# Memory products ordered by the half of the keys and values that they read, and three value blocks open at once

## The chip, the cores and the metric

The kernel runs on one NeuronCore of a Trainium2 chip. The metric is the device time of one execution in microseconds (us); three runs of the kernel before gave 1373.69, 1375.38 and 1381.63 us, with a median of 1375.38 us. The engines are TensorE (PE for the products, PEld for the weight loads that go with them), VectorE (DVE), ScalarE (ACT), GpSimd (POOL) and SyncE (SP), which here only issues DMAs.

## The reference, cut to what matters

One decoder layer over 1024 tokens of width 1024. It has a state-space mixer (S5), gated linear attention, cross-attention into 256 memory tokens, and a squared-ReLU MLP. The change touches the cross-attention alone:

```python
mem_n = layer_norm(mem, mem_ln_g, mem_ln_b)          # (256, 1024)
kv = mem_n @ w_kv
k = kv[..., :D_MODEL].reshape(bsz, MEM_LEN, MEM_HEADS, MEM_HEAD_DIM)   # 4 heads of 256
v = kv[..., D_MODEL:].reshape(bsz, MEM_LEN, MEM_HEADS, MEM_HEAD_DIM)
s = jnp.einsum('blhd,bmhd->bhlm', q, k) * (MEM_HEAD_DIM ** -0.5)       # q = x @ w_q
p = jax.nn.softmax(s, axis=-1)
o = jnp.einsum('bhlm,bmhd->blhd', p, v)
return o @ w_o
```

## The kernel before, in words

The memory does not depend on the tokens, so the kernel folds it into two matrices before it needs them. For each head it computes `A = w_q k^T` (stored in DRAM as `a_d`) and `VW = v w_o` (stored as `vw_d`); the attention later is `softmax(h A) VW`. The generator `mem_stream` does this head by head: it transposes `w_q` (`mem_wqT`), projects the memory to the keys (`mem_proj`), forms A in four blocks of 256 rows, projects the memory to the values (`mem_proj` again) and forms VW in four blocks of 128 x 512.

Every product that needs float32 precision is made of three. `split` cuts a matrix into a high half (ACT copies it in a shorter format) and a low half (DVE or POOL subtracts the high half from the source); `mm3` then adds high x high, high x low and low x high in one PSUM bank. Keys and values come out of `mem_proj` in the tile `kvT`: ACT writes the high half first, and DVE writes the low half behind it, both from the same PSUM bank. So the low half is late by whatever DVE has in front of it.

PSUM banks come from `bank(tag)`. Tag `"d"` has three of them, handed out in turn; a bank is free again when the last reader of its previous contents is done. The projection to the values has one of the three, and its last reader is the DVE subtraction that makes the low half.

The engines run their instructions in program order, each engine its own. That order is set when the program is built: a list scheduler takes instructions from the code as they become ready by its own estimate, so an edit in one place moves others near it, on every engine.

Head 0 runs at the start of the kernel. Around it the tokens are normalised and transposed, eight tiles of 128 tokens (`embed`: DVE, ACT and POOL share a layer norm, PE transposes, ACT and DVE split into `h0T`), each followed by a block of 24 products (`z_block`). DVE also has a long chain of tiny instructions on `prm` and `par` (128 x 16 and the like), which works out the coefficients of S5. Heads 1 to 3 run much later, mixed with the products of the gated unit and of the linear attention.

The lines that matter below: `mm3` (L168 to L171), `split` (L157 to L163), `mem_proj` (L352), `mem_stream` (L385).

Of the kernel before, what the change touches and what calls it, by code (L numbers as in the profile page):

```python
# [7 lines left out]
F32 = mybir.dt.float32  # L8
# [9 lines left out]
P = 128  # L18
# [63 lines left out]
def hybrid_layer(  # L82
# [8 lines left out]
    nc = tc.nc  # L91
# [3 lines left out]
    PE = nc.tensor  # L95

    x, mem, out = x[0], mem[0], out[0]
# [12 lines left out]
    vw_d = dram.tile([D, D], F32, name="vw_d")  # L110
# [10 lines left out]
    stage = ctx.enter_context(tc.tile_pool(name="stage", bufs=2))  # L121
    psp = ctx.enter_context(tc.tile_pool(name="psp", bufs=2, space=PSUM))

    def slot(name, shape, dtype=F32):
        return arena.tile(shape, dtype, tag="s", name=name)

    def bank(tag="d", shape=(P, 512)):
        return psp.tile(list(shape), F32, tag=tag, bufs={"d": 3, "s": 3, "g": 2}[tag], name="ps_" + tag)
# [26 lines left out]
    def act(o, i, f=AF.Copy, **kw):  # L155
        A.activation(out=o, in_=i, func=f, **kw)  # L156
# [7 lines left out]
            stt(V, lo, src, scale, hi.bitcast(F32), ALU.mult, ALU.subtract)  # L164

    P3 = ((0, 0), (0, 1), (1, 0))

    def mm3(o, lhs, rhs, first, last, more=False):  # L168

        for n, (i, j) in enumerate(P3):  # L170
            PE.matmul(o, lhs(i), rhs(j), start=first and n == 0, stop=last and n == 2, skip_group_check=more)  # L171
# [26 lines left out]
    def eng(bits, i):  # L198
        return V if bits >> i & 1 else G


    def weight(src, shape, e=nc.vector, hl=None):

        raw = rawp.tile(shape, F32, tag="raw", name="raw")
        nc.sync.dma_start(out=raw, in_=src)
        if hl is None:
            hl = wp.tile([P, 2] + list(shape[1:]), F32R, tag="w", name="hl")
        split(hl[:, 0], hl[:, 1], raw, e=e)
        return hl
# [57 lines left out]
    prm_s = slot("prm", [P, 4096])  # L267
# [20 lines left out]
    for b in range(4):  # L288
        z = (b + 1) % 3 * 512 + 512
        t = mrow[:, 0:2, :].rearrange("p a n -> p (a n)")[:, z:z + 512].rearrange("p (k m) -> p k m", k=2)  # L290
        for j in range(2):
# [3 lines left out]
            else:  # L295
# [11 lines left out]
                  in_=lst[64:80, :].unsqueeze(2).to_broadcast([16, 2, 64]))  # L307
# [41 lines left out]
    def mem_w(c0):  # L349
        bits = {0: MW, D: MV0}.get(c0, MV1 if c0 >= D else MW1)  # L350
        return [weight(w_mkv[kk * 512:(kk + 1) * 512, c0:c0 + 256].rearrange("(k p) n -> p k n", p=P), [P, 4, 256],
                       eng(bits, kk))  # L352
                for kk in range(2)]

    def mem_proj(ws):
        ps = bank("d", (P, 2, MEM))
        for dk in range(2):
            for k in range(8):
                mm3(ps[:, dk, :], lambda i: ws[k // 4][:, i, k % 4, dk * P:(dk + 1) * P],
                    lambda j: mnT[:, j, k, :], k == 0, k == 7)  # L360
            yield 2.6
        o = stage.tile([P, 2, 2, MEM], F32R, tag="kv", bufs=1, name="kvT")
        split(o[:, 0], o[:, 1], ps)
        return o

    def mem_load(h):
        ws = mem_w(h * 256)
        raws = []
        for ch in range(2):
            raw = rawp.tile([P, 4, 256], F32, tag="raw", name="wq")  # L370
            nc.sync.dma_start(out=raw, in_=w_mq[ch * 512:(ch + 1) * 512, h * 256:(h + 1) * 256]
                              .rearrange("(k p) n -> p k n", p=P))
            raws.append(raw)
        return ws, raws

    def mem_wqT(raw, tag):
        wq = wp.tile([P, 2, 2, 512], F32R, tag="w", name="wqT")
        for dk in range(2):
            ps = bank(tag, (P, 4, P))
            for ck in range(4):  # L380
                PE.transpose(ps[:, ck, :], raw[:, ck, dk * P:(dk + 1) * P], ident)
            split(wq[:, 0, dk, :], wq[:, 1, dk, :], ps.rearrange("p a c -> p (a c)"))
        return wq

    def mem_stream(heads, tag, room=None):  # L385
        nxt = mem_load(heads[0])
        yield 0
        for h in heads:
            ws, raws = nxt
            wq = [mem_wqT(raws[0], tag)]  # L390
            yield 0.9
            kT = yield from mem_proj(ws)
            wq.append(mem_wqT(raws[1], tag))
            ws = mem_w(D + h * 256)
            yield 0.9
            for r0 in range(0, D, 256):
                ps = bank("d", (P, 2, MEM))
                for c in range(2):
                    ck = r0 // P + c
                    for dk in range(2):  # L400
                        mm3(ps[:, c, :], lambda i: wq[ck // 4][:, i, dk, ck % 4 * P:(ck % 4 + 1) * P],
                            lambda j: kT[:, j, dk, :], dk == 0, dk == 1)
                st = stage.tile([P, 2, MEM], F32, tag="rt", bufs=3, name="ast")
                act(st, ps)
                nc.scalar.dma_start(out=a_d[r0:r0 + 256, h * 256:(h + 1) * 256].rearrange("(c p) m -> p c m", p=P),
                                  in_=st)
                yield 1.3
            wo = [weight(w_mo[h * 256:(h + 1) * 256, n * 512:(n + 1) * 512].rearrange("(k p) n -> p k n", p=P),
                         [P, 2, 512], eng(MO1 if room is None else MO0, n), None if room is None else room[:, n]) for n in range(2)]
            vT = yield from mem_proj(ws)  # L410
            if h != heads[-1]:
                nxt = mem_load(h + 1)
            yield 0
            for n in range(2):
                for mt in range(2):
                    ps = bank()
                    for dk in range(2):
                        mm3(ps, lambda i: vT[:, i, dk, mt * P:(mt + 1) * P], lambda j: wo[n][:, j, dk, :],
                            dk == 0, dk == 1)
                    z = (0, 512, 1792, 3456)[2 * n + mt]  # L420
                    st = (prm_s[:, z:z + 512] if room is not None and z
                          else stage.tile([P, 512], F32, tag="rt", bufs=3, name="vst"))
                    act(st, ps)
                    r0 = h * 256 + mt * P
                    nc.scalar.dma_start(out=vw_d[r0:r0 + P, n * 512:(n + 1) * 512], in_=st)
                    yield 1.3


    def z_block(w, tok, t, epi):
# [15 lines left out]
    def load_x(tk):  # L445
        nc.sync.dma_start(out=xs[tk // 4][:, tk % 4, :], in_=x[tk * P:(tk + 1) * P, :])

    fill = Filler(mem_stream([0], "g", slot("wo0", [P, 2, 2, 2, 512], F32R)))
    fill.run(F1)
    xs = [slot("xs0", [P, 4, D])]  # L450
# [86 lines left out]
    for th in range(2):  # L537
        po = bank()
        for k in range(8):
            for j in range(2):  # L540
                PE.matmul(po[0:32, :], wg[:, k, :], h0(k, j)[:, th * 512:(th + 1) * 512],
                          start=k == 0 and j == 0, stop=k == 7 and j == 1)
# [48 lines left out]
    def exp_parts(z):  # L591

        zc, n, r, em, sc, kk = etmp
        ex, ex1 = pt(), pt()
        ts(e, zc, z, 88.0, -90.0, ALU.min, ALU.max)
        ts(e, n, zc, LOG2E, MAGIC, ALU.mult, ALU.add)
        ts(e, n, n, MAGIC, op0=ALU.subtract)
        stt(e, r, n, -LN2H, zc, ALU.mult, ALU.add)
        stt(e, r, n, -LN2L, r, ALU.mult, ALU.add)
        ts(e, em, r, 1.0 / 5040)  # L600
        for c in (1.0 / 720, 1.0 / 120, 1.0 / 24, 1.0 / 6, 0.5, 1.0):
            stt(e, em, em, c, r, ALU.add, ALU.mult)
        ts(e, kk, n, 127.0, 0.0, ALU.add, ALU.max)
        ts(e, sc.bitcast(I32), kk, 8388608.0)
        stt(e, ex, em, 1.0, sc, ALU.add, ALU.mult)
        tt(e, em, em, sc, ALU.mult)
        stt(e, ex1, sc, -1.0, em, ALU.add, ALU.add)
        return ex, ex1
# [9 lines left out]
    step, _ = exp_parts(ls)  # L618
# [35 lines left out]
    n = 1  # L654
# [18 lines left out]
    for Et, cnt in ((E0, 16), (E1, 8)):  # L673
        G.memset(Et[:, 0, 0, :], 1.0)
        G.memset(Et[:, 1, 0, :], 0.0)
        n = 1
# [226 lines left out]
    def z_stream():  # L903
# [24 lines left out]
        for t in range(NT):  # L928
# [8 lines left out]
            yield 5.1  # L937

    mem_rest = mem_stream([1, 2, 3], "d")
    fill = Filler(z_stream(), mem_rest)  # L940
    fill.run(10)
# [48 lines left out]
    class Act:  # L990
# [8 lines left out]
        def lhs(self, k, i, t):  # L999
            return self(k // 4, t // 4)[:, i, k % 4, (t % 4) * P:(t % 4 + 1) * P]  # L1000

        def rhs(self, k, j, th):
            return self(k // 4, th)[:, j, k % 4, :]
# [406 lines left out]
    for _ in range(2):  # L1410
        z = wp.tile([P, 2, 2, 512], F32R, tag="w", name="w1q")
# [339 lines left out]
```

## Time and profile before

| | |
|---|---|
| median of three runs | 1375.38 us (1373.69 to 1381.63) |
| profiled execution | 1376.45 us, of which the span from first to last instruction is 1374.4 us |
| mean granted TensorE clock | 0.990 of 2.4 GHz |
| busy: PE, DVE, ACT, POOL | 97%, 70%, 41%, 30% of the span |

PE is busy nearly always, so time can be gained or lost only where it waits, or where its clock is at the lower level. The times in the sections below are microseconds from the start of the span.

### The profile page before, as it was taken

What the parts mean: (1) busy time and instruction counts of PE and PEld (TensorE: products, weight loads), DVE (VectorE), ACT (ScalarE), POOL (GpSimd) and SP (SyncE); (2) the same over time, 40 slices, a digit from 0 to 9 for tenths busy, and PEclk for the clock granted to TensorE, in tenths of its full rate; (3) what the DMA queues carried; (4) which work ended last, traced back from release to release, by engine and by line L of the source; (5) the groups of instructions that cost most, each with busy time, mean ns of one, the idle gap of its engine ahead of it and who ended that gap; (6) DMA issues with size and microseconds to landing.
All of it is one profiled execution on the core that took longest, in us unless ns stands there. A gap on an engine that the chain in (4) does not pass through costs nothing. (4 is left out here: it accounts for less than half of the span.)

```text
span 1374.4 us, 18808 instructions
## 1 busy us (share of the span) xinstructions
PE 1333.9 (97%) x6824; PEld 1108.2 (81%) x6824; DVE 968.6 (70%) x1713; ACT 569.6 (41%) x950; POOL 410.6 (30%) x315
## 2 busy tenths in 40 slices
PE   6799999999999999999999999999999999999997
PEld 6576788788898888788888788888887888888886
DVE  8999788756965379744379866665556576678785
ACT  4434433242545245333023754545556343344441
POOL 1654243311524123000013134443342143003363
PEclk9899999999999999999999999999999999999999
DMA  9832342543666220300112557644446983335332
GB/s 301 269 123 85 114 122 52 174 153 118 241 210 214 61 78 17 122 31 25 38 46 86 183 172 242 199 155 159 159 163 231 320 315 130 106 108 160 131 108 92
DMA packets 155512, 199.81 MB, mean 145 GB/s; under 512 B 16294, under 2 KB 86044, under 8 KB 155292
## 3 DMA queue, kind: packets, MB, share of 16 engines
q1 hardware_dynamic: 143536, 179.44, 40.1%
q10 hardware_dynamic: 11884, 19.17, 3.8%
q8 instruction: 54, 0.88, 0.3%
q14 instruction: 38, 0.31, 0.1%
HBM read 140.38 MB, written 58.20 MB: 144 GB/s over the span
## 5 line engine op out<-in xcount | busy, mean ns | idle before, releaser
L171 PE MATMUL ps_d<-xt,w1q 128*128 128x512 f32 x576 | 137.3, 389 | 0.7 <-DVE hid L150 0.7
L171 PEld LDWEIGHTS ps_d<-xt,w1q 128*128 128x128 f32 x576 | 108.1, 188 | 23.5 <-DVE hid L150 1.1
L171 PE MATMUL ps_s<-cell 128*128 128x512 f32 x432 | 113.0, 389 | 0.0
L171 PE MATMUL ps_d<-cell 128*128 128x512 f32 x432 | 106.0, 389 | 0.5 <-DVE hid L150 0.5
L171 PEld LDWEIGHTS ps_d<-cell 128*128 128x128 f32 x432 | 81.0, 188 | 17.7 <-DVE hid L150 0.9
L171 PEld LDWEIGHTS ps_s<-cell 128*128 128x128 f32 x432 | 81.1, 188 | 16.8
L156 ACT ACTIVATE hl<-raw 128x1024 fp32r<-128x1024 f32 x62 | 65.4, 1064 | 69.2 <-PE ps_d L171 63.1
L171 PE MATMUL ps_d<-hl,y 128*128 128x512 f32 x384 | 92.4, 395 | 0.0
L171 PE MATMUL ps_d<-hl,h0T 128*128 128x512 f32 x384 | 92.1, 397 | 0.3 <-DVE h0T L150 0.3
L171 PE MATMUL ps_g<-xb,w1q 128*128 128x512 f32 x384 | 92.1, 391 | 0.0
L171 PE MATMUL ps_d<-h0T,hl 128*128 128x512 f32 x384 | 90.8, 393 | 0.6 <-DVE hl L150 0.6
L171 PE MATMUL ps_d<-hl,p 128*128 128x512 f32 x384 | 89.0, 391 | 0.0
L171 PEld LDWEIGHTS ps_d<-h0T,hl 128*128 128x128 f32 x384 | 71.2, 188 | 19.9 <-issue 3.0
L156 ACT ACTIVATE hid<-hid 128x512 f32<-128x512 f32 x112 | 70.8, 632 | 39.0 <-DVE hid L150 37.2
L171 PEld LDWEIGHTS ps_d<-hl,h0T 128*128 128x128 f32 x384 | 72.0, 190 | 16.1 <-DVE h0T L150 0.7
L150 DVE TENSOR_TENSOR cell<-ha,cell 128x1024 fp32r<-128x1024 f32 x56 | 82.3, 1471 | 3.0 <-ACT cell L156 3.0
L171 PEld LDWEIGHTS ps_d<-hl,p 128*128 128x128 f32 x384 | 71.6, 188 | 14.6
L171 PEld LDWEIGHTS ps_g<-xb,w1q 128*128 128x128 f32 x384 | 71.5, 188 | 14.6
L150 DVE TENSOR_TENSOR hl<-raw,hl 128x1024 fp32r<-128x1024 f32 x50 | 68.5, 1381 | 20.7 <-ACT hl L156 20.2
L171 PEld LDWEIGHTS ps_d<-hl,y 128*128 128x128 f32 x384 | 70.7, 188 | 14.6 <-issue 0.3
L156 ACT ACTIVATE w1q<-raw 128x512 fp32r<-128x512 f32 x80 | 50.1, 629 | 69.9 <-PE ps_d L171 27.3
L150 POOL TENSOR_TENSOR hl<-raw,hl 128x1024 fp32r<-128x1024 f32 x12 | 33.8, 2823 | 144.0 <-ACT hl L156 144.0
(296 smaller groups left out, 2798.0 us busy)
## 6 DMA issues: line engine op xcount, KB each, us to landing
g_d<-hid SPq DMA_DIRECT2D x112, 256.0 KB
ha<-g_d SPq DMA_DIRECT2D x56, 512.0 KB
raw<-in_w_ff_dram SPq DMA_DIRECT2D x40, 512.0 KB
b<-in_w_ff_dram SPq DMA_DIRECT2D x32, 512.0 KB
raw<-in_w_mkv_dram SPq DMA_DIRECT2D x16, 512.0 KB
raw<-in_w_in_dram SPq DMA_DIRECT2D x16, 512.0 KB
wq<-in_w_mq_dram SPq DMA_DIRECT2D x8, 512.0 KB
xs<-in_x_dram SPq DMA_DIRECT2D x8, 512.0 KB
```

What stands on the lines that cost most here:

```text
L150: e.tensor_tensor(out=o, in0=a, in1=b, op=op)
L156: A.activation(out=o, in_=i, func=f, **kw)
L171: PE.matmul(o, lhs(i), rhs(j), start=first and n == 0, stop=last and n == 2, skip_group_check=more)
```

## The change

The four blocks of A and the four blocks of VW keep their products and their sums; the order of the products inside changes. `HI_FIRST` lists, for each block, first the four products that read the high half of `kvT` and then the two that read the low half. For VW the first three blocks are opened together: their twelve high products stand in front, then their six low products, then the fourth block alone. Three banks of tag `"d"` are therefore held at once. The numbers in `yield` are the amounts by which other work is interleaved.

```diff
+    HI_FIRST = ((0, 0, 0), (0, 1, 0), (1, 0, 0), (1, 1, 0), (0, 0, 1), (1, 0, 1))
...
                 for c in range(2):
                     ck = r0 // P + c
-                    for dk in range(2):
-                        mm3(ps[:, c, :], lambda i: wq[ck // 4][:, i, dk, ck % 4 * P:(ck % 4 + 1) * P],
-                            lambda j: kT[:, j, dk, :], dk == 0, dk == 1)
+                    for n, (dk, i, j) in enumerate(HI_FIRST):
+                        PE.matmul(ps[:, c, :], wq[ck // 4][:, i, dk, ck % 4 * P:(ck % 4 + 1) * P], kT[:, j, dk, :],
+                                  start=n == 0, stop=n == 5)
...
-            for n in range(2):
-                for mt in range(2):
-                    ps = bank()
-                    for dk in range(2):
-                        mm3(ps, lambda i: vT[:, i, dk, mt * P:(mt + 1) * P], lambda j: wo[n][:, j, dk, :],
-                            dk == 0, dk == 1)
-                    z = (0, 512, 1792, 3456)[2 * n + mt]
...
-                    yield 1.3
+            blocks_ = [(n, mt) for n in range(2) for mt in range(2)]
+            for part in (blocks_[:3], blocks_[3:]):
+                pss = [bank() for _ in part]
+                for lo in range(2):
+                    for ps, (n, mt) in zip(pss, part):
+                        for z, (dk, j, i) in enumerate(HI_FIRST):
+                            if z // 4 == lo:
+                                PE.matmul(ps, vT[:, i, dk, mt * P:(mt + 1) * P], wo[n][:, j, dk, :],
+                                          start=z == 0, stop=z == 5)
+                        if lo:
+                            z = (0, 512, 1792, 3456)[2 * n + mt]
...
+                            yield 0.5 if len(part) > 1 else 1.3
+                    if not lo:
+                        yield 0.9 * len(part) if len(part) > 1 else 0
```

On PE, the value products of head 0 stood like this before (`ps_d_432` to `ps_d_460` are the four blocks, `kvT_429` the values, `wo0_189` the two halves of `w_o`, and the brackets name the engines whose work a row waits for):

```order
L171 MATMUL ps_d_432<-wo0_189,kvT_429 128x512 [waits Activation_49]
L171 MATMUL ps_d_432<-wo0_189,kvT_429 128x512 [waits Pool_49]
L171 MATMUL ps_d_442<-wo0_189,kvT_429 128x512 [waits PE_49]
L171 MATMUL ps_d_442<-wo0_189,kvT_429 128x512
L171 MATMUL ps_d_432<-wo0_189,kvT_429 128x512 [waits DVE_49]
L171 MATMUL ps_d_432<-wo0_189,kvT_429 128x512 x3
L171 MATMUL ps_d_442<-wo0_189,kvT_429 128x512 x4
L171 MATMUL ps_d_451<-wo0_189,kvT_429 128x512 [waits PE_49]
```

In the changed program the blocks are `ps_d_432`, `ps_d_433`, `ps_d_434` and, behind these rows, `ps_d_460`:

```order
L425 MATMUL ps_d_432<-wo0_189,kvT_429 128x512 [waits Activation_49]
L425 MATMUL ps_d_432<-wo0_189,kvT_429 128x512 [waits Pool_49]
L425 MATMUL ps_d_432<-wo0_189,kvT_429 128x512 x2
L425 MATMUL ps_d_433<-wo0_189,kvT_429 128x512 [waits PE_49]
L425 MATMUL ps_d_433<-wo0_189,kvT_429 128x512 x3
L425 MATMUL ps_d_434<-wo0_189,kvT_429 128x512 [waits DVE_49]
L425 MATMUL ps_d_434<-wo0_189,kvT_429 128x512 x3
L425 MATMUL ps_d_432<-wo0_189,kvT_429 128x512 x2
```

The wait for DVE moved from behind the fourth product to behind the eighth. It stands at the first product of the third block, a product of high halves, and no later row waits for DVE again: the third block gets the bank out of which DVE makes the low half. Head 1 has the same two rows, with two products before the wait where it was, and eight now.

On DVE, the place in head 0 where the low half of the values is made, and what follows on the tokens (`hl_481` is a weight split, `h0T` the split token tiles, `tq` the steps of an inverse square root, `prm` the S5 chain), before:

```order
L150 TENSOR_TENSOR kvT_429<-ps_d_380,kvT_429 128x512
L150 TENSOR_TENSOR hl_481<-raw_479,hl_481 128x1024
L150 TENSOR_TENSOR h0T01_337<-ps_s_514,h0T00_336 128x4x128
...
L153 SCALAR_TENSOR_TENSOR prm_101<-prm_101 128x16 x9
L150 TENSOR_TENSOR h0T11_339<-ps_s_521,h0T10_338 128x4x128
L153 SCALAR_TENSOR_TENSOR prm_101<-prm_101 128x16 x6
```

And now:

```order
L150 TENSOR_TENSOR hl_481<-raw_479,hl_481 128x1024
L150 TENSOR_TENSOR kvT_429<-ps_d_380,kvT_429 128x512
...
L150 TENSOR_TENSOR h0T01_337<-ps_s_514,h0T00_336 128x4x128
L147 TENSOR_SCALAR tq_685<-tq_685 128x1
L153 SCALAR_TENSOR_TENSOR tq_685<-tq_685 128x1 x6
L153 SCALAR_TENSOR_TENSOR tq_685<-mv_684,tq_685 128x1
L153 SCALAR_TENSOR_TENSOR xs0_268<-xs0_268,tq_685,row_301 128x512
L150 TENSOR_TENSOR h0T11_339<-ps_s_521,h0T10_338 128x4x128
```

The weight split now stands ahead of the low half, and most of the `prm` chain moved from the middle of the token tiles to behind the seventh of them. The 376 DVE instructions that precede the weight splits `hl_1089` and `hl_1094`, with which the products behind the tokens begin, are the same ones in both programs; only their order differs.

On SP, the loads around the second half of the tokens (`xs1_489`) were:

```order
L205 DMA raw_484<-in_w_in_dram 128x2x512
L205 DMA raw_1082<-in_w_in_dram 128x2x512
L205 DMA raw_1087<-in_w_in_dram 128x2x512
L205 DMA raw_1092<-in_w_in_dram 128x2x512
L583 DMA prm_101<-in_ssm_d_dram 16x16x1 x2
L708 DMA prm_101<-in_ssm_b_re_dram 128x16x16
L708 DMA prm_101<-in_ssm_b_im_dram 128x16x16
L446 DMA xs1_489<-in_x_dram 128x1024 x4
```

They are now:

```order
L207 DMA raw_1082<-in_w_in_dram 128x2x512
L207 DMA raw_1087<-in_w_in_dram 128x2x512
L207 DMA raw_1092<-in_w_in_dram 128x2x512
L207 DMA raw_1097<-in_w_in_dram 128x2x512
L593 DMA prm_101<-in_ssm_d_dram 16x16x1 x2
L718 DMA prm_101<-in_ssm_b_re_dram 128x16x16
L718 DMA prm_101<-in_ssm_b_im_dram 128x16x16
L456 DMA xs1_489<-in_x_dram 128x1024 x4
```

One more weight load (`raw_1097`) stands ahead of the tokens. The load of `b_im` overwrites inputs of small PE products (64 x 64); of their sixteen, seven stood ahead of the value products of head 0, and now thirteen do.

## Rows read from the trace of the kernel before

**Rows 1.** The page, busy time and share of the span of each engine.

```profile
PE 1333.9 (97%) x6824; PEld 1108.2 (81%) x6824; DVE 968.6 (70%) x1713; ACT 569.6 (41%) x950; POOL 410.6 (30%) x315
```

**Rows 2.** Waits of PE, whole span: us in total, times, longest us.

```profile
PE ps_d L171 <- DVE kvT L150: 7.3, 3, 5.5
...
PE ps_s L259 <- POOL xs L150: 3.7, 3, 2.4
PE ps_d L171 <- ACT kvT L156: 2.9, 2, 2.0
```

**Rows 3.** Windows: length, busy us per engine (instructions), granted PE clock, DMA share, GB/s.

```profile
34.50:60.00 25.50, 17.78 (x104) 13.99 (x103) 25.19 (x95) 11.83 (x21) 14.87 (x8) 0.80 0.82 244
60.00:90.00 30.00, 26.29 (x124) 21.26 (x123) 29.74 (x69) 11.32 (x19) 16.24 (x12) 0.94 0.50 188
90.00:121.70 31.70, 31.09 (x146) 22.93 (x144) 29.71 (x140) 10.90 (x17) 13.21 (x19) 1.00 0.23 84
...
146.00:200.00 54.00, 54.00 (x335) 43.23 (x334) 40.61 (x76) 23.51 (x41) 17.13 (x21) 1.00 0.43 127
```

**Rows 4.** Timeline of PE, head 0: start, us, instructions, idle before and its releaser.

```profile
24.05 5.78 PE L171 MATMUL ps_d<-kvT,wqT 128*128 128x256 f32 x46 [0.23 <-DVE kvT L150]
...
38.73 1.19 PE L171 MATMUL ps_d<-wo,kvT 128*128 128x512 f32 x4 [1.99 <-ACT kvT L156]
45.40 7.35 PE L171 MATMUL ps_d<-wo,kvT 128*128 128x512 f32 x20 [5.47 <-DVE kvT L150]
```

**Rows 5.** Timeline of ACT ahead of the high half of the values.

```profile
32.72 0.60 ACT L156 ACTIVATE ast<-ps_d 128x512 f32<-128x512 f32 x1 [2.52 <-DMA a_d<-ast]
...
37.14 1.06 ACT L156 ACTIVATE hl<-raw 128x1024 fp32r<-128x1024 f32 x1 [0.42 <-DMA raw<-in_w_in_dram]
```

**Rows 6.** Timeline of DVE, head 0 to the products behind the tokens.

```profile
36.04 3.38 DVE L150 TENSOR_TENSOR wo<-raw,wo 128x1024 fp32r<-128x1024 f32 x1
39.34 2.32 DVE L153 SCALAR_TENSOR_TENSOR tq<-tq 128x1 f32<-128x1 f32 x1
...
44.67 0.68 DVE L150 TENSOR_TENSOR kvT<-ps_d,kvT 128x512 fp32r<-128x512 f32 x1
45.27 1.69 DVE L150 TENSOR_TENSOR hl<-raw,hl 128x1024 fp32r<-128x1024 f32 x1
...
54.64 3.10 DVE L153 SCALAR_TENSOR_TENSOR prm<-prm 128x16 f32<-128x16 f32 x9
...
117.02 4.56 DVE L150 TENSOR_TENSOR hl<-raw,hl 128x1024 fp32r<-128x1024 f32 x2
```

**Rows 7.** Timeline of POOL in the same stretch.

```profile
35.85 5.79 POOL L150 TENSOR_TENSOR hl<-raw,hl 128x1024 fp32r<-128x1024 f32 x2 [3.60 <-ACT hl L156]
...
117.67 2.83 POOL L150 TENSOR_TENSOR hl<-raw,hl 128x1024 fp32r<-128x1024 f32 x1 [4.90 <-ACT hl L156]
```

**Rows 8.** Timeline of PE, token tiles and the products behind them.

```profile
78.31 1.11 PE L259 MATMUL ps_s<-ident,xs 128*128 128x128 f32 x4 [2.35 <-POOL xs L150]
79.08 6.88 PE L171 MATMUL ps_d<-hl,h0T 128*128 128x512 f32 x24
...
86.59 5.73 PE L171 MATMUL ps_d<-hl,h0T 128*128 128x512 f32 x24
...
121.64 2.56 PE L171 MATMUL ps_d<-h0T,hl 128*128 128x512 f32 x10 [0.61 <-DVE hl L150]
```

**Rows 9.** Timeline of PE, value products of heads 1 and 2.

```profile
358.81 0.73 PE L171 MATMUL ps_d<-hl,kvT 128*128 128x512 f32 x2 [0.86 <-ACT kvT L156]
361.13 5.53 PE L171 MATMUL ps_d<-hl,kvT 128*128 128x512 f32 x16 [1.58 <-DVE kvT L150]
...
395.11 3.03 PE L171 MATMUL ps_d<-hl,kvT 128*128 128x512 f32 x12
```

**Rows 10.** Windows as in rows 3, around stretches in which PE was idle.

```profile
361.00:365.00 4.00, 3.87 (x10) 3.04 (x11) 4.00 (x6) 0.60 (x1) 0.62 (x1) 0.57 0.62 218
...
548.00:554.00 6.00, 4.62 (x25) 3.66 (x24) 6.00 (x11) 3.70 (x5) 0.33 (x1) 1.00 0.54 176
```

**Rows 11.** Waits of the SP queue from 0 to 130 us: us, times, longest.

```profile
SPq L708 <- PE ps_g L500: 5.0, 1, 5.0
```

More of the change, by code (lines that the diff above doesn't have):

```diff
@@ L413, in mem_stream @@
             yield 0
-            for n in range(2):
-                for mt in range(2):
-                    ps = bank()
-                    for dk in range(2):
-                        mm3(ps, lambda i: vT[:, i, dk, mt * P:(mt + 1) * P], lambda j: wo[n][:, j, dk, :],
-                            dk == 0, dk == 1)
-                    z = (0, 512, 1792, 3456)[2 * n + mt]
[L421 to L425, printed above, removed]
-                    yield 1.3
+            blocks_ = [(n, mt) for n in range(2) for mt in range(2)]
[9 more added lines that the diff above has]
+                            z = (0, 512, 1792, 3456)[2 * n + mt]
+                            st = (prm_s[:, z:z + 512] if room is not None and z
+                                  else stage.tile([P, 512], F32, tag="rt", bufs=3, name="vst"))
+                            act(st, ps)
+                            r0 = h * 256 + mt * P
+                            nc.scalar.dma_start(out=vw_d[r0:r0 + P, n * 512:(n + 1) * 512], in_=st)
+                            yield 0.5 if len(part) > 1 else 1.3
+                    if not lo:
+                        yield 0.9 * len(part) if len(part) > 1 else 0
     def z_block(w, tok, t, epi):
```

## The prediction

> **What bounds the kernel now.** I read the page first: PE is busy for 97% of the span, DVE for 70%, ACT and POOL for less [rows 1]. So the change can only act on the 3% in which PE is idle, or on its clock. Next I read PE's waits by what ended them [rows 2]. The memory products (`mm3` with `kvT`) waited 7.3 us for DVE in three waits and 2.9 us for ACT in two; the transposes of the token tiles waited 3.7 us for POOL in three. Each list is short, so each wait can be found on the timeline. The three for DVE are 0.23 us at the scores of head 0 and 5.47 us at its values [rows 4], and 1.58 us at the values of head 1; those of head 2 ran as twelve products in 3.03 us without a stop [rows 9]. The two for ACT are 1.99 us [rows 4] and 0.86 us [rows 9]. Only heads 0 and 1 can therefore give anything.
>
> Then I read the windows, to see which engine sets the pace where the waits lie. From 34.5 to 60 us DVE was busy for 25.19 of 25.50 us and PE for 17.78; from 60 to 90 DVE for 29.74 of 30.00; from 90 to 121.7 DVE for 29.71 of 31.70. From 146 to 200 it is the other way round: PE 54.00 of 54.00, DVE 40.61 [rows 3]. So up to about 121.6 us, where PE waits a last time for DVE's split `hl` (0.61 us) [rows 8], DVE bounds the kernel, and PE behind that. This is the reading on which most depends: time that PE wins in head 0 is kept only as far as DVE reaches the split at 121.6 earlier too.
>
> **Scores.** In head 0 the six products now begin with four that need only the high half. That can take away the 0.23 us. ACT, next in line, was itself held for a weight from DRAM (0.42 us at 37.14) and, ahead of that, for a store of A (2.52 us at 32.72) [rows 5]; these waits don't move with PE. I count nothing.
>
> **Values, head 0.** Before, four products ran, then PE waited for the low half. Twelve high products now stand in front, but the first product of the third block already waits for DVE, because its bank is the one out of which DVE makes the low half: eight run, not twelve. So four products more lie ahead of the wait. Behind it they took 7.35/20 = 0.37 us each [rows 4], at the lower clock level; at the upper one 24 took 5.73, or 0.239 each [rows 8]. The gain is 4 x 0.37 = 1.5 us; its bounds are 4 x 0.239 = 1.0 and, with the 0.23 of the scores, 1.7.
>
> From this goes what the low half is late. DVE wrote it from 44.67 to 45.35; a weight split, 1.69 us, stood behind it and stands ahead now [rows 6]. Against that, the split of `wo` (3.38 us at 36.04) and a `tq` step of 128 x 1 (2.32 us at 39.34) ran while POOL worked from 35.85 to 41.64 [rows 6, 7]. Set against 1.69 us for a split of the same shape, and 3.10/9 = 0.34 us for a tiny step [rows 6], they lost 1.7 + 2.0 = 3.7 us. The `wo` split now comes earlier in DVE's order, so it may start before POOL does. The low half is thus between 1.7 us late (nothing recovered) and 3.7 - 1.7 = 2.0 us early. I take 0.5 us late, which says that 1.2 of the 3.7 us come back: POOL's work stays as long, and what DVE does beside it now is again tiny steps and splits. Head 0: 1.5 - 0.5 = 1.0 us for PE.
>
> The Trainium skill ("SBUF — State Buffer", section "Who interferes with whom") says that a DVE instruction with two SBUF inputs and a GpSimd instruction that reads SBUF lock the same ports, and that whichever issues first keeps them for the whole instruction. The trace agrees in this one place, where DVE's split began 0.19 us behind POOL's and took twice as long; by the rule the split that now starts first would lose nothing and the low half would come up to 2.0 us early, which makes head 0 worth 3.5 us instead of 1.0, as in the fourth case below.
>
> **Token tiles.** PE can win more here. Most of the `prm` chain moves from the middle of the tiles to behind the seventh, and the load of `b_im`, for which SP's queue stood 5.0 us behind PE's small products [rows 11], finds thirteen of the sixteen done ahead of the values; the tokens' second half is queued behind it and comes earlier by most of that, less the one weight load that is now ahead. So the wait of 2.35 us at 78.31 should shrink, and with it the lower clock behind it: 24 products took 6.88 there and 5.73 later [rows 8], so 1.15 us. With head 0 PE would be some 1.0 + 1.5 to 1.0 + 3.5 = 2.5 to 4.5 us earlier at 121.
>
> **What DVE lets through.** The same 376 instructions stand ahead of the pair of splits there, so DVE wins only through less idleness or shorter stalls. Its idle time from 34.5 to 121.7 was 0.31 + 0.26 + 1.99 = 2.6 us [rows 3], no more to win than that. The `prm` steps filled time in which it would have waited for PE and ACT: with them moved, the cost is from nothing to the fifteen steps that the order shows, 15 x 0.34 = 5.2 us. I take 1.0, nearer nothing, because DVE had a backlog nearly everywhere. The pair itself took 4.56 us while POOL worked from 117.67 [rows 6, 7]; two unhindered splits are 2 x 1.69 = 3.4, and with POOL's split earlier, as PE and ACT are, I expect that 1.2 us back, beside the 1.2 us that come back near the low half. So DVE is 1.2 + 1.2 - 1.0 = 1.4 us earlier, PE waits for it longer than the 0.61 us of before, and the start gives **1.4 us**; the bounds are 5.2 late and 3.7 + 1.2 = 4.9 early.
>
> **Values, head 1.** Two products ran before the wait of 1.58 us; eight will. Six more at 0.239 are 1.4 us, so the wait falls to about 0.15. The pause also cost clock: it was 0.57 from 361 to 365 [rows 10], and sixteen products took 5.53 [rows 9] against 16 x 0.239 = 3.82, so 1.7 us. Between 548 and 554 PE was idle for 6.00 - 4.62 = 1.38 us, and the clock stayed at 1.00 [rows 10]; so the remaining 0.86 us for ACT with some tenths behind it should not lower it. Together 1.4 + 1.6 = **3.0 us**; 1.4 if the dip stays. Nothing is in front of DVE here that was not before.
>
> **Edits costed at nothing.** Three banks are open at once, and the evictions come in a bunch. The fourth block needs the first block's bank; between them lie four low products, 4 x 0.239 = 0.96 us, and an eviction is 0.60 us [rows 5]. That hides it; without that cover it is 0.60 us in each of four heads, 2.4 us. Heads 2 and 3 have no wait to lose [rows 9] and gain nothing.
>
> **The sum.** 1.4 + 3.0 = 4.4 us. The profiled execution took 1376.45 us, so 1372.05; it lies 1.07 above the median of the three runs, whose spread is 7.9 us. I name **1372.0 us**.
>
> **Rivals.**
> (a) The likeliest, as above, with a gain of 2 to 7 us (1369.5 to 1374.5): chance 0.52.
> (b) DVE eats the start: the low half is 1.5 us or more late, as its new place behind a split allows, and head 0 gains nothing; DVE reaches the pair at its old time or up to 2 us later, and only head 1 is left with 1.4 to 3.0. That the change doesn't do what it says for head 0 belongs here: the third block's wait is for the same DVE instruction as before. It is for this that DVE is full in all three windows [rows 3]; against it is the loss to POOL in the same stretch, which has room to shrink. 1376.45 + 2 - 1.4 = 1377 at most, 1374.5 at least: 0.25.
> (c) Slower: the `prm` chain is missing as cover. DVE stands idle for PE and ACT at the tiles, does the chain later, and comes to the pair at 121.6 up to 5.2 us late; every microsecond costs PE one. With head 1 at 1.4 it decides from 1.4 us late on, and gives up to 1376.45 + 5.2 - 1.4 = 1380.2. For it: the chain is the only work of DVE there that waits for nobody; against it: DVE was idle for only 2.6 us in 87, so it seldom needed cover. 0.08.
> (d) Larger gain: stalls under POOL go, DVE is 4.9 us early or more, and PE keeps the tile waits too: 3.5 for head 0, 2.35 + 1.15 for the tiles, 3.0 for head 1, which is 10.0, or 1366.4; with DVE's cap, 4.9 + 3.0 = 7.9, or 1368.6. For it: the split that starts ahead of POOL's; against it: POOL is as busy as before and meets other instructions. 0.15.
>
> **How the numbers follow.** The range reaches from 1367.5, the middle of (d), to 1378.5, the near half of (c): outside are some 0.08 of (d), 0.05 of (c), and a few hundredths for the spread of runs. 0.5% is 6.9 us, about what a measurement of this kernel can tell from no change. Only (d) goes beyond that downward, with a little of (a): 0.13 faster. Upward it takes (c) with several microseconds more than its bound, or a shifted set of runs: 0.05. Within it: 0.82.
>
> **What would show it.** Right, in the profile after: eight value products in one run near 39 us, then a wait for `kvT` of 3.5 to 5 us; a wait for DVE of 1 to 3 us at the split near 120, with DVE done there near 120.3; in head 1 a wait of at most 0.4 us and a clock near 1.00 behind it; unbroken values in heads 2 and 3. Wrong: the split near 120 done after 122 (then the chain was cover), or before 118 (then POOL's stalls went); a clock in head 1 that still falls (1.6 us less); a wait of the fourth block for ACT. If several stretches behind 400 us differ, I missed something that the order of all engines brings.

## The result, and the profile after

| | before | after |
|---|---|---|
| median, runs of both on one chip | 1375.45 us | 1385.35 us (1384.58 to 1387.89, 6 runs) |
| after / before | | 1.0066, 95% interval 1.0046 to 1.0086 |
| profiled execution, span | 1376.45, 1374.4 us | 1385.49, 1383.5 us |

The change makes the kernel slower by 0.66%, 9.9 us; faster by some 3 us was forecast. The span grew by 9.1 us. Where, is read from work that stands in both programs in the same place. PE's first product of 32 x 512 behind the tokens starts at 124.13 us before and 134.23 after (+10.1); the projection ahead of head 1's values at 349.85 and 360.93 (+11.1); the second half of the projection behind them at 375.23 and 385.00 (+9.8); the end is +9.1. So the loss is made in the first 134 us, head 1 gives 1.3 us back, and nothing else moves by more than about a microsecond.

The waits of PE in the whole span of the changed kernel, to be set beside [rows 2]:

```profile
PE ps_d L425 <- DVE kvT L150: 7.6, 2, 7.4
PE ps_d L173 <- DVE hl L150: 6.0, 1, 6.0
...
PE ps_d L425 <- ACT kvT L156: 3.3, 2, 2.5
PE ps_s L261 <- POOL xs L150: 2.3, 2, 2.0
```

The three waits for the low halves have become two, but the sum has not shrunk, and the wait for the split `hl` behind the tokens, 0.6 us before, is 6.0. PE's timeline shows both, to be set beside [rows 4, 8] (start, us, instruction, idle before and its releaser):

```profile
38.76 2.12 PE L425 MATMUL ps_d<-wo,kvT 128*128 128x512 f32 x8 [2.48 <-ACT kvT L156]
48.25 4.08 PE L425 MATMUL ps_d<-wo,kvT 128*128 128x512 f32 x10 [7.37 <-DVE kvT L150]
...
119.71 1.97 PE L173 MATMUL ps_d<-h0T,hl 128*128 128x512 f32 x8
127.69 6.61 PE L173 MATMUL ps_d<-h0T,hl 128*128 128x512 f32 x16 [6.00 <-DVE hl L150]
```

Eight products do stand ahead of the first wait, which nevertheless ends 2.85 us later than before (48.25 against 45.40). PE makes nearly all of that good: its transposes at 98.92 are 0.4 us behind those at 98.50 before. Then it waits 1.38 us for DVE's `h0T` at 100.91, and at 119.71 it is 2.0 us behind the 117.69 of [rows 8]. There it waits 6.00 us instead of 0.61, and the clock falls: the sixteen products behind the wait take 6.61 us instead of 16 x 0.239 = 3.8. Their window (length, then busy us and count of PE, PEld, DVE, ACT, POOL, the granted clock, DMA) has a clock of 0.55, near the lower level of 1.2 GHz, half of full speed:

```profile
127.69:134.20 6.51, 6.51 (x16) 4.88 (x16) 6.51 (x19) 0.00 (x0) 3.81 (x5) 0.55 0.76 207
```

That is the whole loss, within 0.1 us of the 10.1 above: 2.0 + 6.0 - 0.6 + 2.8 = 10.2 us.

DVE is what both waits end on. Its timeline, beside [rows 6]:

```profile
34.53 1.23 DVE L150 TENSOR_TENSOR wo<-raw,wo 128x1024 fp32r<-128x1024 f32 x1 [0.51 <-ACT wo L156]
35.67 4.66 DVE L153 SCALAR_TENSOR_TENSOR tq<-tq 128x1 f32<-128x1 f32 x2
...
43.16 0.68 DVE L233 BATCH_NORM_STATS2 st<-xs 128x6 f32<-128x512 f32 x1
43.76 1.77 DVE L153 SCALAR_TENSOR_TENSOR tq<-tq 128x1 f32<-128x1 f32 x1
...
47.51 0.68 DVE L150 TENSOR_TENSOR kvT<-ps_d,kvT 128x512 fp32r<-128x512 f32 x1
...
56.29 0.69 DVE L150 TENSOR_TENSOR h0T<-ps_s,h0T 128x512 fp32r<-128x512 f32 x1 [3.71 <-ACT h0T L156]
...
119.72 2.50 DVE L150 TENSOR_TENSOR par<-par,prm 128x32 f32<-128x32 f32 x2
...
126.42 2.92 DVE L150 TENSOR_TENSOR hl<-raw,hl 128x1024 fp32r<-128x1024 f32 x2
```

And POOL's, beside [rows 7]:

```profile
35.52 4.79 POOL L150 TENSOR_TENSOR hl<-raw,hl 128x1024 fp32r<-128x1024 f32 x2 [3.84 <-ACT hl L156]
40.28 2.94 POOL L150 TENSOR_TENSOR xs<-xs,row 128x512 f32<-128x512 f32 x2
43.18 2.34 POOL L150 TENSOR_TENSOR hl<-raw,hl 128x1024 fp32r<-128x1024 f32 x1
...
119.69 2.40 POOL L150 TENSOR_TENSOR hl<-raw,hl 128x1024 fp32r<-128x1024 f32 x1 [4.16 <-ACT hl L156]
```

Two steps on 128 x 1 take 4.66 us beside two POOL splits of 4.79 us together, two of 128 x 32 take 2.50 us beside one of 2.40. Between 34.5 us and the pair of splits DVE does nearly the same instructions in both kernels. The windows of before and of after:

```profile
34.50:117.00 82.50, 71.07 (x352) 55.12 (x351) 79.94 (x300) 31.61 (x54) 40.29 (x35) 0.92 0.50 170
```

```profile
34.50:126.40 91.90, 72.60 (x356) 55.51 (x354) 86.91 (x298) 33.23 (x56) 42.33 (x40) 0.94 0.44 147
```

DVE needs 86.91 us for 298 instructions, where it needed 79.94 for 300: **7.0 us more for the same work**. Its idle time, what is left of the windows, went from 2.56 to 4.99 us, **2.4 us more**; 3.71 of the 4.99 are the one wait at 56.29. Together they are the 9.4 us by which the pair starts later (126.42 against 117.02).

### The profile page after: what moved, and what is told of

Same layout as the page of the kernel before. It is cut to its first block, busy times and chain, and to the rows that moved or that the text cites. A ratio compares the mean times of both kernels' runs of the same rounds, so it can differ in the third digit from the quotient of the medians.

```text
span 1383.5 us, 18802 instructions
## 1 busy us (share of the span) xinstructions
PE 1334.8 (96%) x6824; PEld 1108.7 (80%) x6824; DVE 972.6 (70%) x1713; ACT 569.3 (41%) x950; POOL 411.6 (30%) x315
## 5 line engine op out<-in xcount | busy, mean ns | idle before, releaser
L150 POOL TENSOR_TENSOR hid<-hid 128x512 f32<-128x512 f32 x32 | 49.8, 1555 | 82.8 <-DVE hid L150 75.8
```

What stands on the lines that cost most here:

```text
L150: e.tensor_tensor(out=o, in0=a, in1=b, op=op)
```

## The experiments

Each ratio is the kernel's time over that of the kernel before on the same chip, with its 95% interval. "Low half" is DVE's `kvT` of head 0's values (44.67 us before, 47.51 after), "pair" the start of the two splits behind the tokens (117.02 and 126.42).

The theories: **O**, the new order of instructions, above all on DVE, makes the start late; **B**, the three open value blocks of head 0 do it. Then, on why DVE is late: **L**, its small steps stand still while POOL's instruction runs, against **W**, it just has more work ahead. And **D**, DVE sets the end of the start stage, against **P**, PE does; **S**, the order on ACT, SP and PE makes the loss.

**Which part of the edit.** Four kernels take the change apart; the code shown is cut, and stands against the changed kernel. `e1_scores_only` keeps the values as before:

```diff
-            for part in (blocks_[:3], blocks_[3:]):
...
+            for n in range(2):
+                for mt in range(2):
+                    ps = bank()
...
+                        mm3(ps, lambda i: vT[:, i, dk, mt * P:(mt + 1) * P], lambda j: wo[n][:, j, dk, :],
```

> Only the order of the products of A changes (all four heads); the values are as before. In the built programs this edit alone brings most of the new order on DVE near head 0. Theory O (the new order of instructions on the other engines costs the time, by stalls of DVE under POOL and by idle time behind the low half): slower by 8 to 12 us than before, DVE's split for the products behind the tokens done near 127 us. Theory B (the three open value blocks of head 0 cost it: the third block's bank and the bunched evictions): within 2 us of before.

Measured: 1.0052 (1.0036 to 1.0067), some 7 us slower, a little less than O expected and far more than B allows. The low half comes at 46.96, the pair at 125.14, and PE waits there 5.5 us:

```profile
118.93 1.98 PE L173 MATMUL ps_d<-h0T,hl 128*128 128x512 f32 x8
126.40 3.89 PE L173 MATMUL ps_d<-h0T,hl 128*128 128x512 f32 x10 [5.50 <-DVE hl L150]
```

`e2_values_only` does the opposite:

```diff
-                    for n, (dk, i, j) in enumerate(HI_FIRST):
-                        PE.matmul(ps[:, c, :], wq[ck // 4][:, i, dk, ck % 4 * P:(ck % 4 + 1) * P], kT[:, j, dk, :],
-                                  start=n == 0, stop=n == 5)
+                    for dk in range(2):
+                        mm3(ps[:, c, :], lambda i: wq[ck // 4][:, i, dk, ck % 4 * P:(ck % 4 + 1) * P],
+                            lambda j: kT[:, j, dk, :], dk == 0, dk == 1)
```

> Only the value blocks change (all four heads); the products of A stand as before, and DVE's order at head 0 is that of before. Theory O: faster than before by 1 to 4 us; eight value products ahead of a wait that ends near 45 us, DVE's split near 121 us as before, and the wait of head 1 nearly gone. Theory B: slower than before by 8 to 12 us.

Measured: 0.9995 (0.9982 to 1.0008). The values do what was wanted of them in place, and it is gone 14 us later. PE's timeline:

```profile
38.74 3.28 PE L424 MATMUL ps_d<-wo,kvT 128*128 128x512 f32 x8 [2.28 <-ACT kvT L156]
43.51 4.01 PE L424 MATMUL ps_d<-wo,kvT 128*128 128x512 f32 x16 [1.48 <-DVE kvT L150]
...
57.46 4.63 PE L173 MATMUL ps_d<-hl,h0T 128*128 128x512 f32 x10 [4.56 <-DVE h0T L150]
```

The wait of 5.47 us [rows 4] is 1.48, and the first transposes behind the values start 5.2 us earlier than before (47.35 against 52.59). Not all of this is the edit's: 1.9 us of it come from the low half, which is earlier here although DVE's order is that of before:

```profile
35.11 1.21 DVE L150 TENSOR_TENSOR wo<-raw,wo 128x1024 fp32r<-128x1024 f32 x1
...
42.77 0.68 DVE L150 TENSOR_TENSOR kvT<-ps_d,kvT 128x512 fp32r<-128x512 f32 x1
```

The split of `wo` began 0.30 us ahead of POOL's split (35.41) and took 1.21 us; before, it began 0.19 us behind and took 3.38 [rows 6, 7]. It went as here in `e3`, `e8` and `e11` below (low half at 43.49, 43.28 and 43.24), and as before in `e9` and `e10` (44.11 and 44.38). So with one order some tenths of a microsecond decide it, and little depends on it at the pair: 116.66 in `e3` and 117.70 in `e8`, against 117.02.

Then ACT stands for a weight transfer, ahead of the token halves that DVE and PE need:

```profile
55.66 0.60 ACT L156 ACTIVATE prm<-ps_g 128x512 f32<-128x512 f32 x1 [5.35 <-DMA raw<-in_w_in_dram]
```

The pair is at 118.02, near the old time. Faster by 1 to 4 us was expected; it is not seen, but the loss of theory B is excluded.

`e3_heads1to3` has both halves of the change behind `if h:`, with the old code for head 0; `e4_head0_only` behind `if not h:`.

```diff
+                if h:
...
+                        for n, (dk, i, j) in enumerate(HI_FIRST):
...
+                else:
...
+                        for dk in range(2):
+                            mm3(ps[:, c, :], lambda i: wq[ck // 4][:, i, dk, ck % 4 * P:(ck % 4 + 1) * P],
```

> The whole change in heads 1 to 3 only; head 0 as before. Both theories: the start is as before, and what is left is head 1: faster by 1.4 us (the wait alone) to 3 us (the clock too). If something else in the later heads costs time, it is slower than before.

> The whole change in head 0 only; heads 1 to 3 as before. Both theories: slower than before by 10 to 12 us, that is the changed kernel without what head 1 gives back. If the loss were made in the later heads, it is within 2 us of before.

Measured: 0.9990 (0.9976 to 1.0003), and 1.0067 (1.0052 to 1.0083). The 1.4 us by which `e3` is faster are the least that was expected of it, and not beyond its interval. The loss is head 0's, and e1 and e2 say of which half: the products of A. The products themselves wait for nothing new; those of A ran without a stop in the changed kernel. But in the program built with them alone the weight split stands ahead of the low half and the chain behind the tokens, as in the changed kernel; in the program built with the values alone DVE's rows up to the pair are, one by one, those of before.

**Why DVE is late.** The next three kernels keep the change and take weight splits from POOL. The constants say which of four splits DVE makes, one bit each. `e5_split3_on_dve` moves one instruction and no other:

```diff
-MWR = 4
+MWR = 12
```

> The changed kernel, with one weight split of the start (the third that POOL made, 2.34 us at 43.18) given to DVE; every other instruction stands in the same order on every engine. Theory L (DVE's tiny steps stand still while POOL's instruction runs): DVE does 1.2 us more work but stands still some 1.6 us less, so the low half of the values comes 0.3 to 0.6 us earlier than 47.51, and the time is within 1 us of the changed kernel. Rival W (DVE is late because it has more work ahead, POOL has no part in it): the low half comes 1.2 us later and the time grows by 1 us.

Measured: 1.0064 (1.0043 to 1.0085), as the changed kernel. The low half comes at 45.38, 2.1 us earlier. The moved split stands behind it:

```profile
46.84 1.22 DVE L150 TENSOR_TENSOR hl<-raw,hl 128x1024 fp32r<-128x1024 f32 x1
```

So DVE has the same work ahead of the low half, and only POOL's split is gone: W, in which POOL has no part, falls. L had the sign right and the size too small, since the expectation counted the 1.2 us ahead of the low half. At the pair, with 1.2 us more of work ahead, DVE is still 1.4 us earlier (124.99).

`e6_splits_on_dve`:

```diff
-MWR = 4
+MWR = 15
```

> The changed kernel, with all three weight splits of the start that POOL made (4.79 and 2.34 us) given to DVE, so that POOL has only the token rows there. Theory L: of the 8.2 us that DVE stood still from 34.5 to 48 us some 6 go, against 3 x 1.2 = 3.6 us more work: the low half comes 1.5 to 3 us earlier than 47.51, and the kernel is 1 to 3 us faster than the changed one. Rival W: the low half comes 3.6 us later, and the kernel is 2 to 4 us slower than the changed one.

Measured: 1.0034 (1.0018 to 1.0050); by the two ratios 0.3% faster than the changed kernel, with DVE doing three splits more. Its timeline:

```profile
34.84 1.21 DVE L150 TENSOR_TENSOR wo<-raw,wo 128x1024 fp32r<-128x1024 f32 x1
...
36.91 2.35 DVE L150 TENSOR_TENSOR hl<-raw,hl 128x1024 fp32r<-128x1024 f32 x2
39.55 0.69 DVE L150 TENSOR_TENSOR kvT<-ps_d,kvT 128x512 fp32r<-128x512 f32 x1 [0.30 <-ACT kvT L156]
...
121.86 2.91 DVE L150 TENSOR_TENSOR hl<-raw,hl 128x1024 fp32r<-128x1024 f32 x2
```

The low half comes 8.0 us earlier, more than expected: the two splits ahead of it run at 1.2 us each, no tiny step is caught, and the new order leaves two of the splits behind it. PE's wait for it is gone:

```profile
39.57 7.15 PE L425 MATMUL ps_d<-wo,kvT 128*128 128x512 f32 x18 [3.03 <-ACT kvT L156]
...
123.13 5.92 PE L173 MATMUL ps_d<-h0T,hl 128*128 128x512 f32 x16 [6.01 <-DVE hl L150]
```

Yet the kernel is slower than before, since the pair is at 121.86 and PE waits 6.01 us there. All that PE won in head 0 is stood out in that one wait.

`e7_u_split_too` adds the split at 119.69:

```diff
-MWU = 7
+MWU = 15
```

> As the kernel before it, with also the weight split that POOL made at 119.69 us given to DVE, where it stands behind the pair for which PE waits. Theory L: the steps ahead of the pair no longer stand still under it (2.50 us for two of some 0.18 each), so the pair comes 2 us earlier, and the kernel is 1 to 2 us faster than the one with three splits on DVE. Rival W: no difference at the pair.

Measured: 1.0042 (1.0028 to 1.0057). The pair is at 119.60, 2.3 us earlier, as L has it, and PE's wait there falls to 3.8 us. The time did not follow: it isn't faster than e6. In the two profiles PE is still 3.5 us earlier than in e6 at the projection of head 1 (352.21 against 355.67), 3.4 us at 757 us and 0.2 us at 1041 us; 2.1 us of this go into four waits for DVE's `w1s` between 846 and 891 us, which e6 does not have. Whether they follow from the edit wasn't tried.

**Two value blocks open, not three.** `e8_values_two_open` has e2's edit with

```diff
-            for part in (blocks_[:3], blocks_[3:]):
+            for part in (blocks_[:2], blocks_[2:]):
```

> The products of A as before; of VW two blocks open at a time instead of three, so that no block of the first round takes the bank of the values. The built order is that of before on DVE, POOL and SP, and the split of a weight on ACT stays behind the four evictions. Theory O (order): faster than before by 1 to 3 us, since eight products stand ahead of the low half in heads 0 and 1, with no wait of ACT for a transfer as in the kernel with three open. If the value products ahead of a wait bring nothing at all: same as before.

Measured: 0.9998 (0.9981 to 1.0015). No block takes the values' bank, and ACT has no wait of 5 us there. PE's wait for the low half is 2.92 us, its transposes start at 49.39 instead of 52.59, and then it stands 3.01 us for `h0T`:

```profile
57.94 4.07 PE L173 MATMUL ps_d<-hl,h0T 128*128 128x512 f32 x10 [3.01 <-DVE h0T L150]
```

DVE reaches that `h0T` at 57.20 (57.67 before), and the pair at 117.70. The 1 to 3 us that were expected are not there: the third block's bank wasn't what kept them away.

**The bound itself.** `e9_extra_dve_work` gives the kernel before eight more DVE instructions whose result nobody uses:

```diff
+    sx = small.tile([P, 2, 6], F32, tag="st", name="sx")
+    for _ in range(8):
+        V.bn_stats(out=sx[:, 0, :], in_=xs[1][:, 3, 0:512])
     wu = [wcols(w_in, 2 * kp, 0, eng(MWU, kp)) for kp in range(4)]
```

> The kernel before, with eight more statistics of 128 x 512 on DVE (0.6 us each beside one another, 4.9 us together), written to a tile that nobody reads; they stand behind the last token tile, ahead of the pair of splits for which PE waited 0.61 us, and every other engine has the order of before. Theory D (DVE sets the end of the start stage): the pair comes 4.5 to 5 us later, PE waits 4.5 to 5.5 us there, and the kernel is 4 to 5 us slower. Rival P (PE sets it, DVE has slack): slower by less than 1.5 us.

Measured: 1.0052 (1.0031 to 1.0074).

```profile
123.36 2.92 DVE L150 TENSOR_TENSOR hl<-raw,hl 128x1024 fp32r<-128x1024 f32 x2
```

```profile
124.63 5.83 PE L171 MATMUL ps_d<-h0T,hl 128*128 128x512 f32 x16 [5.51 <-DVE hl L150]
130.39 1.12 PE L555 MATMUL ps_s<-prm 32*128 32x512 f32 x2
```

The pair is 6.3 us late, not 4.9, and the product of 32 x 512 starts 6.3 us later than before (130.39 against 124.13). P falls. PE had nothing changed ahead of it.

**The chain as cover.** `e11_before_chain_late` changes the order of the kernel before, and no part of the change is in it:

```diff
+        if tk == 5:
+            held = traced(V)
...
+    hold = ExitStack()
+    hold.enter_context(behind(held))
     step, _ = exp_parts(ls)
...
     mag, mag1 = exp_parts(zre)
+    hold.close()
```

> The kernel before, with the chain of tiny DVE steps (the two exponentials of S5, some fifty steps on 128 x 16) held behind the token tiles, about where the changed kernel has most of it. PE and SP keep their whole order, ACT and POOL theirs but for a few rows behind the stage. Theory O, in its part on cover (the chain filled time in which DVE waits): DVE stands idle for 3 to 4 us near 52 us, the pair of splits comes 4 to 9 us later than 117.02, and the kernel is 4 to 9 us slower. Rival S (the changed order on ACT, SP and PE makes the loss, and DVE's chain may lie anywhere): the pair within 1.5 us of 117.02, the time within 2 us of before.

Measured: 1.0037 (1.0025 to 1.0050). DVE's timeline:

```profile
53.63 0.69 DVE L150 TENSOR_TENSOR h0T<-ps_s,h0T 128x512 fp32r<-128x512 f32 x1 [3.02 <-ACT h0T L156]
...
59.93 1.95 DVE L231 BATCH_NORM_STATS2 st<-xs 128x6 f32<-128x512 f32 x3 [4.04 <-DMA xs<-in_x_dram]
...
120.50 1.22 DVE L150 TENSOR_TENSOR hl<-raw,hl 128x1024 fp32r<-128x1024 f32 x1
```

It stands idle for 3.02 us near 52 and another 4.04 for the second half of the tokens. Up to the pair it is idle for 10.0 of 86.0 us, 7.5 us more than before:

```profile
34.50:120.50 86.00, 73.68 (x359) 56.97 (x357) 75.98 (x264) 34.16 (x56) 41.97 (x37) 0.92 0.47 161
```

The pair comes 3.5 us later than 117.02, a little less than the 4 expected and no more than that because 264 instructions stand ahead of it here, 36 fewer than before. PE, which comes there 2.2 us earlier than before, waits for 4.27 us:

```profile
115.53 1.98 PE L171 MATMUL ps_d<-h0T,hl 128*128 128x512 f32 x8
121.77 6.44 PE L171 MATMUL ps_d<-h0T,hl 128*128 128x512 f32 x16 [4.27 <-DVE hl L150]
```

S falls, in that the chain may not lie anywhere: its place makes a loss of 0.37% while PE and SP keep the order of before. That is no share of the 0.66%: the wait of 4.04 us is not in the changed kernel, whose DVE has only 2.4 us more of idle time. Whether the new order on ACT, SP and PE adds something to the loss isn't shown.

`e12_after_chain_hoisted` is the changed kernel with that code moved ahead of the loop over the tiles 3 to 7 (moved whole, so its diff shows nothing more).

> The changed kernel, with the code of the same chain written ahead of the second half of the token tiles, so that the scheduler puts more of it between the fourth and the sixth tile instead of behind the seventh; PE and SP keep their order. Theory O: the idle time at 52 us stays, since the chain still starts behind it, so the pair gains at most 2 us of the 9.4 and the kernel is 0 to 2 us faster than the changed one. Rival S: the pair within 1 us of 126.42.

Measured: 1.0066 (1.0048 to 1.0085), as the changed kernel. The idle time at 52 stays (4.18 us before the `h0T` at 56.88), as expected, and the pair is at 128.01, 1.6 us later and not earlier, which neither theory has. A chain brought forward that still begins behind the gap covers nothing.

**A better version?** `e10_heads1to3_u_split` is e3 with `MWU = 15`.

> The change in heads 1 to 3 only, and the weight split that POOL made beside the pair near 118 us given to DVE, behind the pair. Theories L and D: the second of the pair ends near 119 instead of 121.2 us, PE waits nothing there, 0.5 to 1 us faster than the change in heads 1 to 3 alone, so 1.5 to 2.5 us faster than before, if the 1.2 us more of DVE work behind the pair delays nothing. If it does: as the change in heads 1 to 3 alone or slower.

Measured: 0.9988 (0.9966 to 1.0009). PE has no wait at the pair, where e3 has one of 0.71 us, and still comes to the product of 32 x 512 no earlier: at 124.03, against 123.79 in e3 and 124.13 before. Its profile shows a wait for DVE's `s` of 1.95 us at 245.68 besides, where e3 has 0.2 in all. It can't be told from e3, nor either of them from the kernel before; none of these experiments gave a version that is faster than before beyond its interval.

## Why the prediction was wrong, by its own steps

**What bounds the kernel** was read rightly, and e9 shows it: DVE up to the pair, and PE behind it, about one for one. e2, e6 and e8 show the other side: the 3 to 6 us by which PE leaves head 0 earlier than before do not make them faster than before.

**The step that failed is "what DVE lets through".** It had DVE 1.4 us earlier at the pair, with bounds of 5.2 late and 4.9 early. It was 9.4 us late, outside both. Two of its three terms were wrong, and the third was right by luck.

First, the stalls under POOL. I took 1.2 us of them to vanish near the low half, because the `wo` split might now start ahead of POOL's. It did, and took 1.23 us instead of 3.38. But POOL's two splits were still there; they caught two steps of 128 x 1 for 4.66 us instead, and the third split, which POOL made at 54.92 before, moved to 43.18 and caught more ahead of the low half. The stalls were not saved but handed to smaller instructions, and the sum grew by 7.0 us: up to the pair the ten `par` steps of 128 x 32 took 5.2 us instead of 1.9, the 39 chain steps on `prm` 10.1 instead of 7.3, the `tq` steps 17.2 instead of 14.8. I had asked which instruction escapes, and not which one stands in its place. The Trainium skill ("SBUF — State Buffer", section "Who interferes with whom") has the rule that an instruction of DVE with at most one SBUF input, outside its two-port modes, does not contend with GpSimd. The trace of before agrees in one place: `h0T` at 46.88, with one input in SBUF and one in PSUM, took 0.68 us inside a POOL instruction that ran from 45.95 to 48.10, while the `tq` step behind it (0.64 us at 47.48) was held to POOL's end. Not every instruction with one input went free: in the changed kernel a `TENSOR_SCALAR` of 128 x 16 took 1.30 us at 57.82, beside POOL's at 57.79, and whether it ran in such a mode no run shows.

The yardsticks of this term were held as well. The split of 1.69 us at 45.27 ran beside POOL's token rows and the nine steps of 3.10 us at 54.64 beside POOL's third split, which [rows 7] leaves out:

```profile
41.59 6.51 POOL L150 TENSOR_TENSOR xs<-xs,row 128x512 f32<-128x512 f32 x4
54.92 2.54 POOL L150 TENSOR_TENSOR hl<-raw,hl 128x1024 fp32r<-128x1024 f32 x1 [6.82 <-ACT hl L156]
```

A split with nothing beside it took 1.2 us, a tiny step at most 0.2. So the two stalls cost some 4.3 us before, not 3.7, and fifteen chain steps some 3 us at most, not 5.2.

Second, the cover. I set 1.0 us for the `prm` chain moved away, since DVE was idle for only 2.6 us in 87. This was the wrong reading of a small number: DVE was seldom idle because the chain filled the gaps, and e11 shows it with the order of PE and SP unchanged: 7.5 us more of idle time. The groups of DVE from 34.5 to 60 us, before and after (count, busy us, mean ns):

```profile
L153 DVE SCALAR_TENSOR_TENSOR prm<-prm 128x16 f32<-128x16 f32 x39 | 7.3, 225 | 0.2
L153 DVE SCALAR_TENSOR_TENSOR tq<-tq 128x1 f32<-128x1 f32 x14 | 5.4, 400 | 0.0
```

```profile
L153 DVE SCALAR_TENSOR_TENSOR tq<-tq 128x1 f32<-128x1 f32 x13 | 9.2, 715 | 0.2
...
L153 DVE SCALAR_TENSOR_TENSOR prm<-prm 128x16 f32<-128x16 f32 x3 | 1.6, 536 | 0.1
L150 DVE TENSOR_TENSOR h0T<-ps_s,h0T 128x512 fp32r<-128x512 f32 x2 | 1.4, 688 | 3.7 <-ACT h0T L156 3.7
```

Thirty-nine steps of the chain ran there before, three after, and 3.7 us of idle time stand in their place.

Third, the pair itself, from which 1.2 us were to come back. It took 2.92 us instead of 4.56, but not for the reason given: POOL's split was not earlier (119.69 against 117.67). The pair was so late that this split had ended ahead of it, and there it had held two `par` steps for 2.50 us.

**The scores** I costed at nothing, 0.23 us of wait aside. By the products that was right; by what the edit does to the program it was the error, because e1 shows that this half alone brings 0.52%, which can't be told from the whole loss.

**The values, head 0:** eight products in one run, then a wait of 3.5 to 5 us; it was 7.37, since the low half came 2.8 us late where 0.5 was taken (bound 1.7).

**The lower clock** behind the new wait (0.55) was in no term: 2.8 us.

**The token tiles** were to give 1.5 to 3.5 us and gave nothing. The load of `b_im` no longer waits 5.0 us for PE, but four weight loads ahead of it took SP from 37.99 to 48.50 (39.44 to 47.39 before), and the tokens' second half was issued from 55.19, not earlier than the 54.15 of before. PE's waits for POOL fell from 3.7 to 2.3 us, the longest from 2.35 to 2.0. But two new waits for DVE, 1.04 us for `prm` and 1.38 us for `h0T`, took as much, and the 24 products behind the longest wait took 7.22 us instead of 6.88.

**Head 1** went as foreseen in its place. PE's timeline and the window behind the wait, beside [rows 9, 10]:

```profile
369.87 2.11 PE L425 MATMUL ps_d<-hl,kvT 128*128 128x512 f32 x8 [0.84 <-ACT kvT L156]
372.21 1.66 PE L425 MATMUL ps_d<-hl,kvT 128*128 128x512 f32 x6 [0.24 <-DVE kvT L150]
...
380.34 0.91 PE L1098 MATMUL ps_g<-g,qk 128*128 128x128 f32 x6 [1.38 <-DVE g L1145]
```

```profile
369.80:373.80 4.00, 3.69 (x15) 2.75 (x16) 4.00 (x4) 0.01 (x1) 2.85 (x2) 1.00 0.93 323
```

The wait of 1.58 us is 0.24, and the clock stays at 1.00. Of the 3.0 us, 1.38 go at once into a wait for DVE at 380.34 that was not there before; net 1.3 us. DVE is full in that window too, which I had not asked of it. Heads 2 and 3, and the evictions of three blocks, cost nothing, as said.

**The rivals.** What happened is (c), given 0.08 and at most 1380.2 us: DVE idle for PE and ACT, the chain done later, the pair late. But the idle time is 2.4 of its 9.4 us; the larger part is the mechanism of (d), with the other sign.

**Left open:** what makes e7 lose its gain on e6 between 757 and 1041 us, and how the loss divides between the chain and the split that moved ahead of the low half; e11 moves the first alone, and no kernel moved the second alone.

## What to carry to other kernels

When a scheduler orders the program, an edit's own cost is the smaller question: the built order should be followed on the engine that bounds the stretch, and each instruction that moved be priced where it now stands, beside what now runs next to it. Little idle time on an engine does not say that the work filling it may be moved. And time that a second engine wins ahead of a bound is worth nothing until the bound moves; in the kernel at hand that is DVE's work, and what it meets of POOL's, in the first 120 us.

## What the runs showed of the hardware that was not expected

A DVE instruction of 128 x 1 or 128 x 32, some 0.15 to 0.2 us by itself, can take as long as what is left of the POOL instruction beside it: two took 4.66 us beside two POOL splits, two took 2.50 us beside one. Which of the two engines begins first is decided by tenths of a microsecond: one and the same split on DVE took 3.38 us where it began 0.19 us behind POOL's and 1.21 us where it began 0.30 us ahead (e2). Taking a split of 2.34 to 2.40 us from POOL made DVE earlier, by 2.1 us at the low half (e5) and 2.3 at the pair (e7), where the moved split stands behind the place; even with its 1.2 us ahead, DVE was 1.4 us earlier at the pair (e5). And eight DVE instructions worth 4.9 us delayed the pair by 6.3 (e9): a `par` step behind them took 2.40 us beside POOL's split at 117.12.
